# Feed-forward: splits traced behind matmuls, modulation rows traced in the third matrix's products alone, sums of weights on DVE

## The chip, the core and the metric

The kernel runs on one core of a Trainium2 chip. A core has a matrix engine (PE, with a track PEld for its weight loads), a vector engine (DVE), a scalar engine (ACT), GpSimd (POOL) and a sync engine (SP) that here only issues transfers; 16 DMA engines move data between HBM and the on-chip memory. Each engine works through its own queue in order, and waits between engines go over semaphores. The metric is the device time of one execution in microseconds (us), as the median of three runs.

## The reference

Two blocks of two layers each work on 512 tokens of width 1024. The change touches the feed-forward of the second block alone, which runs once per layer `l`. The modulation `mod` of the second layer has 48 columns of 128 numbers; the kernel computes them beside the first layer's feed-forward.

```
mod = (c_act @ ada_w[l] + ada_b[l])[:, None, :]
sh1, sc1, g1, sh2, sc2, g2 = jnp.split(mod, 6, axis=-1)
...
h = rmsnorm_2(x, norm_ffn_g[l]) * (1.0 + sc2) + sh2
f = (jax.nn.silu(h @ ffn_w1[l]) * (h @ ffn_w3[l])) @ ffn_w2[l]
x = x + g2 * f
```

## The kernel before

**Products in three parts.** All products keep float32 precision: each operand is cut into a rounded high part and the rest, and three matmuls are accumulated (high times high, high times low, low times high). A weight tile of 128 by 1024 is loaded to `wraw` by SP, its high part `whi` is made by ACT, and its low part `wlo` by DVE, which subtracts. `Weights` does this along a plan: `load` issues a transfer as soon as a buffer is free, `cut` makes the two parts, and `next` hands the next tile to the products and cuts a few tiles ahead (`depth`, 4 in the feed-forward).

**The feed-forward** (`ffn`). The 22 tiles of the hidden width stand in three groups (`FGROUPS`: tiles 0 to 7, 8 to 15, 16 to 21). For each group the first and third weight matrices (`ffn_w1`, `ffn_w3`) give the hidden tiles `G`, and the second (`ffn_w2`, the "third matrix" of the title, products `w2p`) adds its share to `x`. Tiles 0 and 1 of the first group are multiplied plainly. All others go in pairs through `seven` (L1501): two hidden tiles by two halves of the tokens by two halves of the width are formed from seven products in place of eight. That takes sums of four quarters of the weights. Of these, 8 operations on 128 by 512 are made per pair, 80 per layer, by POOL: `sums12` (L139, L140) writes `wsum`, `sums34` (L147, L148) overwrites parts of `wraw`. Each pair then cuts its weights in seven steps: six of 128 by 1024 (L162 on ACT, L170 on DVE) and one of two halves (L166). ACT copies partial results out of PSUM (`sp`, L1522), and DVE adds them (L1594, L1602), which also sets a PSUM bank free for the next product. A layer has ten pairs: three, four and three.

**Modulation of the second layer** (`ada2_gen`, L480). In the first layer's feed-forward, 48 weight tiles of 128 by 1024 are loaded to `adab` (three buffers), and DVE multiplies each by a broadcast vector and sums along the row. One step of this generator is asked for after each pair and at five of sixteen places of the third matrix's products. SP issues these loads in the same queue as the weights (L477 and L119).

**What sets the order.** The code is traced once; a scheduler then orders each engine's queue, by the place in the trace and by when its own model of the program has an instruction ready. `issue_after(ins)` makes the instructions of a block that belong to the engine of `ins` stand behind `ins` in that engine's queue; it says nothing on instructions of another engine. Blocks around `next(ada)` hang on a matmul, and trace instructions for DVE and for a DMA queue.

Of the kernel before, what the change touches and what calls it, by code (L numbers as in the profile page):

```python
# [14 lines left out]
OP = mybir.AluOpType  # L15
# [60 lines left out]
class Weights:  # L76
# [4 lines left out]

    def __init__(self, nc, raw, split, plan, bufs):
        self.nc, self.raw, self.split, self.bufs = nc, raw, split, bufs
        self.loads, self.cuts, self.sums = [], [], []
# [48 lines left out]
    def sums12(self, n, kc):  # L133

        self.load(n + 2)
        G, w = self.nc.gpsimd, kc * 128
        a, b = self.tiles[n], self.tiles[n + 1]
        st = self.extra.tile([128, 2, w], F32, tag="wsum", bufs=2, name="wsum")
        G.tensor_tensor(st[:, 1], b[:, :w], b[:, w:2 * w], op=OP.add)  # L139
        G.tensor_tensor(st[:, 0], st[:, 1], a[:, :w], op=OP.subtract)  # L140
        self.st[n] = st

    def sums34(self, n, kc):

        G, w = self.nc.gpsimd, kc * 128
        a, b = self.tiles[n], self.tiles[n + 1]
        G.tensor_tensor(a[:, :w], a[:, :w], b[:, :w], op=OP.subtract)  # L147
        G.tensor_tensor(a[:, w:2 * w], a[:, w:2 * w], self.st[n][:, 0], op=OP.subtract)  # L148

# [66 lines left out]
    def next(self, n=None):  # L216
        at = self.n_use
        self.cut(at + (n or self.depth))
        self.load(len(self.loads))
        while self.extra and self.sums and self.sums[0][0] <= at:  # L220
            _, f, m, kc = self.sums.pop(0)
            f(m, kc)
        return self.ready.pop(0)[1:]
# [53 lines left out]
class Kern:  # L277
# [4 lines left out]
    def mm3(self, ps, hi, lo, xh, xl, start, stop):  # L282
        mm = self.nc.tensor.matmul
        mm(ps, hi, xh, start=start, stop=False)  # L284
        mm(ps, hi, xl, start=False, stop=False)  # L285
        return mm(ps, lo, xh, start=False, stop=stop).ins  # L286

# [14 lines left out]
    def run(self):  # L302
        tc, nc, a = self.tc, self.nc, self.a
        with ExitStack() as ctx:
# [11 lines left out]
            self.hx = [hp.tile([128, 8, N], F32R, name=f"hx{i}") for i in range(2)]  # L316
            self.W = Weights(nc, self.wraw, self.wsp, self.weight_plan(), 4)
            self.block1(ctx)
# [134 lines left out]
    def ada2_gen(self, l, bufs=None):  # L453
# [19 lines left out]
        ws = []  # L473
        for f in range(48):
            while len(ws) < min(len(bufs) if bufs else 1, 48 - f):
                w = tile()
                nc.sync.dma_start(w, a["ada_wt2"][l, f + len(ws)])  # L477
                ws.append(w)
# [40 lines left out]
    def dense_halves(self, h, outs):  # L519

        w = [self.W.next(self.W.depth - i) for i in range(len(outs))]
        for o in HALVES:
# [825 lines left out]
class Block2:  # L1348
# [155 lines left out]
    def seven(self, pool, banks):  # L1504
# [7 lines left out]
        def product(ps, b, start):  # L1512
            hi, lo = K.W.next()
            for k in range(4):
                mm(ps, hi[:, k, :], b[0][:, k, :], start=k == 0 and start, stop=False, skip_group_check=True)  # L1515
                mm(ps, hi[:, k, :], b[1][:, k, :], start=False, stop=False, skip_group_check=True)  # L1516
                self.mm_last = mm(ps, lo[:, k, :], b[0][:, k, :], start=False, stop=k == 3, skip_group_check=True).ins  # L1517
                self.step()
# [26 lines left out]
    def ffn(self, l, s):  # L1545
# [18 lines left out]
        for gi, (f0, f1) in enumerate(FGROUPS):  # L1564
            G = [gp.tile([128, 8, N], F32R, tag=f"g{i}", name=f"g{i}") for i in range(2)]
            f = f0
            while f < f1:
                if f < FPLAIN:
                    if f:
                        p1, p3 = self.dense("d"), self.dense("pt")  # L1570
                    else:
                        p1, p3 = (K.pt("fa", "dps") for _ in range(2))
                        for _ in K.dense_halves(self.h, (p1, p3)):
                            self.step()
                    sl = big()
                    A.activation(sl, p1, AF.Silu)
# [32 lines left out]
                K.split(G[0][:, f - f0 + 1, :], G[1][:, f - f0 + 1, :], sl[1])  # L1609
                with self.tc.issue_after(self.mm_last):  # L1610
                    next(ada, None)
                f += 2
# [801 lines left out]
```

## Time and profile before

| | |
|---|---|
| median of three runs | 2543.09 us (2541.26 to 2546.3) |
| profiled execution, its own time | 2536.63 us |
| its span | 2534.8 us |
| PE busy in the span | 2363.8 us, 93% |
| DVE busy | 1934.3 us, 76% |
| ACT busy | 1358.1 us, 54% |
| POOL busy | 508.8 us, 20% |
| HBM read | 255.82 MB, 105 GB/s over the span |

The feed-forward of layer 0 lies from about 1527 to 1914 us of the span, that of layer 1 from about 2165 to 2523 us. The pairs of layer 0 lie from 1554 to 1633, 1678 to 1772 and 1817 to 1878 us, those of layer 1 from 2193 to 2257, 2302 to 2383 and 2427 to 2487 us; the third matrix's products stand between and behind them. A share of busy time is an average over all stages; a stage's limit is read from its own stretch, by which engine is never idle there and by what PE waits for. Matmuls are pipelined, so PE is shown busy also when its clock is lowered.

### The profile page before, as it was taken

The numbers are of one execution on the slowest core, as the hardware profiler recorded it, in microseconds if no ns is written. First come the engines' busy times: TensorE is split into PE (matmuls) and PEld (weight loads), VectorE is DVE, ScalarE is ACT, GpSimd is POOL, SyncE is SP. The second block draws the span as 40 slices with busy tenths as digits, with TensorE's granted clock in tenths as the row PEclk, the third lists the DMA queues.
The fourth block names the chain that finished last, engine by engine and source line by source line (L and its number), as shares of the span: only waits on it lengthen the run. The fifth ranks groups of instructions, "written<-read, shape, count | busy, mean of one in ns | idle before, by whom it ended". The sixth has DMA issues, their size and how long they took to land. (4 is left out here: it accounts for less than half of the span.)

```text
span 2534.8 us, 37905 instructions
## 1 busy us (share of the span) xinstructions
PE 2363.8 (93%) x14392; PEld 2035.2 (80%) x14392; DVE 1934.3 (76%) x3109; ACT 1358.1 (54%) x2656; POOL 508.8 (20%) x366
## 2 busy tenths in 40 slices
PE   7899999999999999999978998898999889899998
PEld 3788888888887888888766777888897578789997
DVE  5778777888367888887589869999477985976765
ACT  4566555667245655577645554435355555544443
POOL 0110000000020000000045105344333520444440
PEclk9999999999999999999988998999999899999999
DMA  6112332234331156523322114674232212232322
GB/s 257 45 55 92 103 101 94 88 98 146 99 95 44 55 176 217 185 76 113 92 72 68 55 59 141 236 255 144 82 100 72 68 56 67 84 125 76 125 72 71
DMA packets 87750, 269.68 MB, mean 106 GB/s; under 512 B 12048, under 2 KB 22544, under 8 KB 87184
## 3 DMA queue, kind: packets, MB, share of 16 engines
q1 hardware_dynamic: 85152, 257.96, 31.4%
q0 software_dynamic: 2416, 9.31, 1.0%
q8 instruction: 113, 1.85, 0.3%
q14 instruction: 69, 0.57, 0.1%
HBM read 255.82 MB, written 11.40 MB: 105 GB/s over the span
## 5 line engine op out<-in xcount | busy, mean ns | idle before, releaser
L284 PE MATMUL dps<-hx,whi 128*128 128x512 f32 (+1 forms) x1040 | 416.1, 400 | 16.2 <-ACT q L1739 5.0
L286 PE MATMUL dps<-hx,wlo 128*128 128x512 f32 (+1 forms) x1040 | 403.9, 388 | 10.9 <-DVE wlo L205 8.5
L285 PE MATMUL dps<-hx,whi 128*128 128x512 f32 (+1 forms) x1040 | 404.3, 389 | 3.2 <-DVE hx L517 2.2
L204 ACT ACTIVATE whi<-wraw 128x1024 fp32r<-128x1024 f32 (+2 forms) x202 | 194.0, 964 | 256.8 <-issue 78.1
L205 DVE TENSOR_TENSOR wlo<-wraw,whi 128x1024 fp32r<-128x1024 f32 (+1 forms) x182 | 225.4, 1239 | 77.4 <-ACT whi L204 75.9
L286 PEld LDWEIGHTS dps<-hx,wlo 128*128 128x128 f32 x1040 | 202.4, 195 | 47.3 <-DVE wlo L205 9.3
L284 PEld LDWEIGHTS dps<-hx,whi 128*128 128x128 f32 x1040 | 203.0, 195 | 45.7 <-DVE t L1762 6.6
L285 PEld LDWEIGHTS dps<-hx,whi 128*128 128x128 f32 x1040 | 202.9, 195 | 28.4 <-DVE hx L517 4.2
L1158 ACT ACTIVATE ph<-PT 128x512 fp32r<-128x512 f32 (+1 forms) x280 | 152.8, 559 | 134.1 <-PE PT L1153 130.7
L1159 DVE TENSOR_TENSOR pl<-PT,ph 128x512 fp32r<-128x512 f32 (+1 forms) x280 | 175.1, 640 | 43.1 <-ACT ph L1158 41.0
L162 ACT ACTIVATE whi<-wraw 128x512 fp32r<-128x512 f32 x200 | 121.0, 626 | 100.9 <-PE w2p L285 35.4
L1141 PE MATMUL Y<-ph,vt 128*128 128x256 f32 (+1 forms) x592 | 161.3, 282 | 6.8 <-DVE T L1175 2.9
L1142 PE MATMUL Y<-pl,vt 128*128 128x256 f32 (+1 forms) x592 | 162.5, 291 | 3.4 <-DVE pl L1159 3.2
L1153 PE MATMUL PT<-ident,P 128*128 128x128 f32 x1024 | 159.5, 275 | 5.9 <-DVE pl L1159 4.0
L1208 POOL DMA_DIRECT2D us<-T x22 | 12.4, 564 | 744.6 <-DVE T L1203 714.2
L284 PE MATMUL w2p<-g,whi 128*128 128x512 f32 (+1 forms) x364 | 140.8, 387 | 1.8 <-ACT sl L1598 1.7
L285 PE MATMUL w2p<-g,whi 128*128 128x512 f32 (+1 forms) x364 | 140.4, 386 | 0.0
L286 PE MATMUL w2p<-g,wlo 128*128 128x512 f32 (+1 forms) x364 | 140.4, 386 | 0.0
L1153 PEld LDWEIGHTS PT<-ident,P 128*128 128x128 f32 x1024 | 118.4, 140 | 23.2 <-DVE pl L1159 9.5
L1141 PEld LDWEIGHTS Y<-ph,vt 128*128 128x128 f32 x592 | 111.7, 189 | 28.6 <-ACT ph L1158 19.7
L170 DVE TENSOR_TENSOR wlo<-wraw,whi 128x1024 fp32r<-128x1024 f32 x80 | 110.3, 1380 | 23.0 <-ACT whi L162 22.7
L1092 PE MATMUL S<-kt,qt 128*128 128x256 f32 (+2 forms) x576 | 125.8, 326 | 1.7 <-DVE nm L1110 0.9
(477 smaller groups left out, 6915.1 us busy)
## 6 DMA issues: line engine op xcount, KB each, us to landing
wraw<-ffn_w SPq DMA_DIRECT2D x120, 512.0 KB, 4.3
wraw<-w_in SPq DMA_DIRECT2D x112, 512.0 KB, 3.5
adaw<-ada_wt SPq DMA_DIRECT2D x80, 512.0 KB, 4.0
adab<-ada_wt SPq DMA_DIRECT2D x48, 512.0 KB, 5.1
wraw<-w_out SPq DMA_DIRECT2D x32, 384.0 KB, 3.1
aw<-ada_w SPq DMA_DIRECT2D x16, 512.0 KB, 10.2
wraw<-w_out SPq DMA_DIRECT2D x16, 512.0 KB, 3.5
bias<-bias_b SPq DMA_DIRECT2D x16, 384.0 KB, 3.5
```

The costliest lines, as they stand in the source:

```text
L162: self.nc.scalar.activation(hi[:, j * w:j * w + w], x, AF.Copy)
L204: s = self.nc.scalar.activation(hi[:, q], t[:, q], AF.Copy)
L205: v = E.tensor_tensor(lo[:, q], t[:, q], fr(hi[:, q]), op=OP.subtract)
L284: mm(ps, hi, xh, start=start, stop=False)
L285: mm(ps, hi, xl, start=False, stop=False)
L286: return mm(ps, lo, xh, start=False, stop=stop).ins
L1092: mm(S[:, so:so + n], Q[:, j, qc], Kt[:, i, ko:ko + n], start=i == 0, stop=i == 1)
L1141: mm(o, v, ph[:, co:co + w], start=b == 0 and n == 0, stop=False, skip_group_check=True)
L1142: mm(o, v, pl[:, co:co + w], start=False, stop=b == len(banks) - 1 and n == len(items) - 1, skip_group_check=True)
L1153: nc.tensor.transpose(pst[:, col:col + 128], ps[t][:, pc:pc + 128], K.ident)
L1158: A.activation(ph[:, :col], pst[:, :col], AF.Copy)
L1159: V.tensor_tensor(pl[:, :col], pst[:, :col], fr(ph[:, :col]), op=OP.subtract)
```

## The change

- The sums of weights (`sums12`, `sums34`) are issued on DVE in place of POOL.
- `next` cuts at most two tiles in front of the products, and the rest of the tiles ahead, with the sums, in a block that hangs on the last matmul. The next loads are traced behind it.
- The first plain tiles cut two tiles in advance and two more at fixed steps of their products.
- The step of the modulation after each pair is gone; the third matrix's products ask for one at six of sixteen places in place of five.
- The modulation's loads in the feed-forward are issued from ACT's queue in place of SP's.

```
@@ -79,8 +79,8 @@
 
 
 
-    def __init__(self, nc, raw, split, plan, bufs):
-        self.nc, self.raw, self.split, self.bufs = nc, raw, split, bufs
+    def __init__(self, K, raw, split, plan, bufs):
+        self.K, self.tc, self.nc, self.raw, self.split, self.bufs = K, K.tc, K.nc, raw, split, bufs
         self.loads, self.cuts, self.sums = [], [], []
         for e in plan:
             n = len(self.loads)
@@ -133,19 +133,19 @@
     def sums12(self, n, kc):
 
         self.load(n + 2)
-        G, w = self.nc.gpsimd, kc * 128
+        V, w = self.nc.vector, kc * 128
         a, b = self.tiles[n], self.tiles[n + 1]
         st = self.extra.tile([128, 2, w], F32, tag="wsum", bufs=2, name="wsum")
-        G.tensor_tensor(st[:, 1], b[:, :w], b[:, w:2 * w], op=OP.add)
-        G.tensor_tensor(st[:, 0], st[:, 1], a[:, :w], op=OP.subtract)
+        V.tensor_tensor(st[:, 1], b[:, :w], b[:, w:2 * w], op=OP.add)
+        V.tensor_tensor(st[:, 0], st[:, 1], a[:, :w], op=OP.subtract)
         self.st[n] = st
 
     def sums34(self, n, kc):
 
-        G, w = self.nc.gpsimd, kc * 128
+        V, w = self.nc.vector, kc * 128
         a, b = self.tiles[n], self.tiles[n + 1]
-        G.tensor_tensor(a[:, :w], a[:, :w], b[:, :w], op=OP.subtract)
-        G.tensor_tensor(a[:, w:2 * w], a[:, w:2 * w], self.st[n][:, 0], op=OP.subtract)
+        V.tensor_tensor(a[:, :w], a[:, :w], b[:, :w], op=OP.subtract)
+        V.tensor_tensor(a[:, w:2 * w], a[:, w:2 * w], self.st[n][:, 0], op=OP.subtract)
 
     def cut_sums(self, at, i, n, kc):
         w = kc * 128
@@ -215,11 +215,17 @@
 
     def next(self, n=None):
         at = self.n_use
-        self.cut(at + (n or self.depth))
+        if self.extra is None:
+            self.cut(at + (n or self.depth))
+        else:
+
+            self.cut(at + min(n or 2, 2))
+            with self.tc.issue_after(self.K.mm_last):
+                self.cut(at + (n or self.depth))
+                while self.sums and self.sums[0][0] <= at:
+                    _, f, m, kc = self.sums.pop(0)
+                    f(m, kc)
         self.load(len(self.loads))
-        while self.extra and self.sums and self.sums[0][0] <= at:
-            _, f, m, kc = self.sums.pop(0)
-            f(m, kc)
         return self.ready.pop(0)[1:]
 
 
@@ -283,7 +289,8 @@
         mm = self.nc.tensor.matmul
         mm(ps, hi, xh, start=start, stop=False)
         mm(ps, hi, xl, start=False, stop=False)
-        return mm(ps, lo, xh, start=False, stop=stop).ins
+        self.mm_last = mm(ps, lo, xh, start=False, stop=stop).ins
+        return self.mm_last
 
     def split(self, hi, lo, src, scale=None):
 
@@ -314,7 +321,7 @@
             self.small = P("small", 3)
             hp = P("hxp")
             self.hx = [hp.tile([128, 8, N], F32R, name=f"hx{i}") for i in range(2)]
-            self.W = Weights(nc, self.wraw, self.wsp, self.weight_plan(), 4)
+            self.W = Weights(self, self.wraw, self.wsp, self.weight_plan(), 4)
             self.block1(ctx)
             self.B2.run()
 
@@ -474,7 +481,7 @@
         for f in range(48):
             while len(ws) < min(len(bufs) if bufs else 1, 48 - f):
                 w = tile()
-                nc.sync.dma_start(w, a["ada_wt2"][l, f + len(ws)])
+                (nc.scalar if bufs else nc.sync).dma_start(w, a["ada_wt2"][l, f + len(ws)])
                 ws.append(w)
             w, o = ws.pop(0), self.junk()
             nc.vector.scalar_tensor_tensor(o, w, 1.0, cb, op0=OP.mult, op1=OP.mult, accum_out=m[:, f:f + 1])
@@ -518,7 +525,7 @@
 
     def dense_halves(self, h, outs):
 
-        w = [self.W.next(self.W.depth - i) for i in range(len(outs))]
+        w = [self.W.next(2 - i) for i in range(len(outs))]
         for o in HALVES:
             for (hi, lo), ps in zip(w, outs):
                 for k in range(8):
@@ -1514,7 +1521,7 @@
             for k in range(4):
                 mm(ps, hi[:, k, :], b[0][:, k, :], start=k == 0 and start, stop=False, skip_group_check=True)
                 mm(ps, hi[:, k, :], b[1][:, k, :], start=False, stop=False, skip_group_check=True)
-                self.mm_last = mm(ps, lo[:, k, :], b[0][:, k, :], start=False, stop=k == 3, skip_group_check=True).ins
+                K.mm_last = mm(ps, lo[:, k, :], b[0][:, k, :], start=False, stop=k == 3, skip_group_check=True).ins
                 self.step()
 
         def copy(src, name):
@@ -1570,8 +1577,11 @@
                         p1, p3 = self.dense("d"), self.dense("pt")
                     else:
                         p1, p3 = (K.pt("fa", "dps") for _ in range(2))
-                        for _ in K.dense_halves(self.h, (p1, p3)):
+                        for i, _ in enumerate(K.dense_halves(self.h, (p1, p3))):
                             self.step()
+                            if i in (17, 25):
+                                with self.tc.issue_after(K.mm_last):
+                                    K.W.cut(K.W.n_split + 1)
                     sl = big()
                     A.activation(sl, p1, AF.Silu)
                     V.tensor_tensor(sl, sl, p3, op=OP.mult)
@@ -1607,8 +1617,6 @@
                     if (t, o) == (0, 1):
                         K.split(G[0][:, f - f0, :], G[1][:, f - f0, :], sl[0])
                 K.split(G[0][:, f - f0 + 1, :], G[1][:, f - f0 + 1, :], sl[1])
-                with self.tc.issue_after(self.mm_last):
-                    next(ada, None)
                 f += 2
 
             if gi == last:
@@ -1620,7 +1628,7 @@
                 for k in range(f1 - f0):
                     v = K.mm3(ps, w[0][:, k, :], w[1][:, k, :], G[0][:, k, o:o + n], G[1][:, k, o:o + n], k == 0,
                               k == f1 - f0 - 1)
-                    if (8 * ct + k) % 16 in (1, 4, 7, 10, 13):
+                    if (8 * ct + k) % 16 in (0, 3, 5, 8, 11, 13):
                         with self.tc.issue_after(v):
                             next(ada, None)
```

What this does to the queues is seen in the order of the instructions. PE's queue has the same order as before. The order on all five queues is row for row the same when the three blocks that hang on a matmul are left out of the changed kernel.

DVE, first pair of layer 0, from the addition that follows the second product to the additions on which PE's last two products wait (`adab`, `junk`: modulation; `wsum`: sums; `wlo`: low parts). Before:

```order
L1594 TENSOR_TENSOR sl<-sfc,sp_15915 128x256
L170 TENSOR_TENSOR wlo<-wraw,whi 128x1024
L467 SCALAR_TENSOR_TENSOR adab<-adab 128x1024
L1602 TENSOR_TENSOR sl<-sy,sp_15949 128x256
L170 TENSOR_TENSOR wlo<-wraw,whi 128x1024
L480 SCALAR_TENSOR_TENSOR junk,mod_9635<-adab 128x1024
L166 TENSOR_TENSOR wlo<-wraw,whi 128x512
L480 SCALAR_TENSOR_TENSOR junk,mod_9635<-adab 128x1024
L166 TENSOR_TENSOR wlo<-wraw,whi 128x512
L480 SCALAR_TENSOR_TENSOR junk,mod_9635<-adab 128x1024
L170 TENSOR_TENSOR wlo<-wraw,whi 128x1024
L1594 TENSOR_TENSOR sl<-sd,sp_15995 128x256
```

And the same place now (L1604 is the former L1594):

```order
L1604 TENSOR_TENSOR sl<-sfc,sp_15915 128x256
L170 TENSOR_TENSOR wlo<-wraw,whi 128x1024
L1612 TENSOR_TENSOR sl<-sy,sp_15949 128x256
L170 TENSOR_TENSOR wlo<-wraw,whi 128x1024
L166 TENSOR_TENSOR wlo<-wraw,whi 128x512 x2
L139 TENSOR_TENSOR wsum<-wraw 128x512
L170 TENSOR_TENSOR wlo<-wraw,whi 128x1024
L140 TENSOR_TENSOR wsum<-wsum,wraw 128x512
L1604 TENSOR_TENSOR sl<-sd,sp_15995 128x256
L1604 TENSOR_TENSOR sl<-spt,sp_15981 128x256
L170 TENSOR_TENSOR wlo<-wraw,whi 128x1024
L139 TENSOR_TENSOR wsum<-wraw 128x512
```

Four modulation operations have left this place, and two sums of half their width stand there; a third sum follows right behind the addition. Counted over DVE's queue between the first addition of one pair and that of the next, the modulation's operations, with the one that prepares the vector, were 5, 6, 7 in the first three pairs, 19 in the products after them, and 6, 6, 0, 0 in the next four. They are now 0, 2, 6, then 18, then 5, 1, 3, 7, and 7 in the products after those. The sums are 8, 8, 0 in the first three pairs, 10 in the products after them, and 6, 8, 8, 0 in the next four.

ACT, fourth pair of layer 0, from its first copy on (`sp`: copies out of PSUM). Before:

```order
L1522 ACTIVATE sp_17024<-sfa 128x256
L162 ACTIVATE whi<-wraw 128x512 x2
L1522 ACTIVATE sp_17058<-sfa 128x256
L162 ACTIVATE whi<-wraw 128x512 x2
L1522 ACTIVATE sp_17090<-sfa 128x256
```

And the same place now:

```order
L1529 ACTIVATE sp_17027<-sfa 128x256
L484 DMA adab<-ada_wt 128x1024
L162 ACTIVATE whi<-wraw 128x512 x2
L1529 ACTIVATE sp_17061<-sfa 128x256
L484 DMA adab<-ada_wt 128x1024
L162 ACTIVATE whi<-wraw 128x512 x2
L1529 ACTIVATE sp_17093<-sfa 128x256
```

A load into one of three buffers stands between two copies of PSUM. Of the 48 loads on ACT, 16 stand among the pairs' copies and 32 in the products of the third matrix (22 after the third pair, 10 after the seventh).

## Rows read from the trace of the kernel before

**Rows 1.** Busy time by stretch: us, engines in turn, clock, DMA share, GB/s.
```profile
1554.00:1633.00 79.00, 66.26 (x504) 64.83 (x503) 77.63 (x93) 39.92 (x80) 38.97 (x20) 0.91 0.60 205
1633.00:1678.00 45.00, 44.69 (x195) 36.50 (x196) 39.26 (x53) 9.86 (x14) 14.29 (x8) 1.00 0.85 285
1678.00:1772.00 94.00, 82.62 (x671) 81.19 (x669) 87.36 (x110) 46.39 (x96) 45.19 (x24) 0.98 0.53 178
1817.00:1878.00 61.00, 60.22 (x505) 59.82 (x504) 50.81 (x56) 34.88 (x72) 25.90 (x14) 1.00 0.32 104
2193.00:2257.00 64.00, 60.54 (x501) 59.65 (x501) 57.49 (x60) 37.69 (x77) 40.12 (x20) 1.00 0.34 109
2302.00:2383.00 81.00, 80.34 (x673) 79.93 (x672) 69.56 (x75) 47.74 (x97) 39.93 (x22) 1.00 0.34 115
```

**Rows 2.** PE groups of the first feed-forward: count, busy, mean ns, idle before, releasers.
```profile
L1515 PE MATMUL sd<-hs,whi 128*128 128x256 f32 x120 | 35.8, 299 | 14.1 <-DVE sl L1594 10.6 <-ACT sp L1522 2.9 <-DVE up L1602 0.5
L1515 PE MATMUL sfa<-hs,whi 128*128 128x256 f32 x120 | 34.9, 291 | 6.5 <-DVE sl L1594 5.7 <-ACT sp L1522 0.8
```

**Rows 3.** Busy time just after the longest of those waits.
```profile
1579.00:1584.00 5.00, 4.54 (x22) 4.54 (x23) 4.11 (x8) 2.90 (x6) 3.63 (x3) 0.52 0.71 262
```

**Rows 4.** Timeline of PE, five waits: start, length, instruction, idle before.
```profile
1535.39 0.39 PE L286 MATMUL dps<-hx,wlo 128*128 128x256 f32 x1 [0.56 <-POOL wlo L205]
...
1555.97 0.39 PE L1517 MATMUL sd<-hx,wlo 128*128 128x256 f32 x1 [1.70 <-DVE wlo L170]
...
1579.46 0.58 PE L1515 MATMUL sd<-hs,whi 128*128 128x256 f32 x1 [4.95 <-DVE sl L1594]
...
2174.78 0.39 PE L286 MATMUL dps<-hx,wlo 128*128 128x256 f32 x1 [1.82 <-POOL wlo L205]
...
2193.94 0.39 PE L1517 MATMUL sd<-hx,wlo 128*128 128x256 f32 x1 [0.94 <-DVE wlo L170]
```

**Rows 5.** DVE groups by shape from 1554 to 1772 us.
```profile
L480 DVE SCALAR_TENSOR_TENSOR junk<-adab 128x1024 bf16<-128x1024 f32 x48 | 67.9, 1414 | 6.4 <-DMA adab<-ada_wt 6.1
L170 DVE TENSOR_TENSOR wlo<-wraw,whi 128x1024 fp32r<-128x1024 f32 x28 | 39.7, 1422 | 3.3 <-ACT whi L162 3.3
L170 DVE TENSOR_TENSOR wlo<-wsum,whi 128x1024 fp32r<-128x1024 f32 x14 | 24.9, 1775 | 0.4 <-ACT whi L162 0.4
L293 DVE TENSOR_TENSOR g<-sl,g 128x512 fp32r<-128x512 f32 x14 | 18.3, 1311 | 0.0
L166 DVE TENSOR_TENSOR wlo<-wraw,whi 128x512 fp32r<-128x512 f32 x14 | 9.0, 679 | 0.0
L1606 DVE TENSOR_TENSOR sl<-sl 128x512 f32<-128x512 f32 x7 | 8.1, 1161 | 0.5
```

**Rows 6.** Timeline of DVE in the first two pairs.
```profile
1574.55 2.31 DVE L480 SCALAR_TENSOR_TENSOR junk<-adab 128x1024 bf16<-128x1024 f32 x1
...
1576.80 2.27 DVE L170 TENSOR_TENSOR wlo<-wraw,whi 128x1024 fp32r<-128x1024 f32 x1
...
1578.99 0.41 DVE L1594 TENSOR_TENSOR sl<-sd,sp 128x256 f32<-128x256 f32 x1
...
1594.10 1.21 DVE L480 SCALAR_TENSOR_TENSOR junk<-adab 128x1024 bf16<-128x1024 f32 x1
...
1599.00 1.28 DVE L166 TENSOR_TENSOR wlo<-wraw,whi 128x512 fp32r<-128x512 f32 x2
```

**Rows 7.** Timeline of POOL: one sum, and one that waits for weights.
```profile
1579.15 1.29 POOL L147 TENSOR_TENSOR wraw<-wraw 128x512 f32<-128x512 f32 x1 [1.16 <-DVE wlo L170]
...
2179.99 1.71 POOL L139 TENSOR_TENSOR wsum<-wraw 128x512 f32<-128x512 f32 x1 [3.55 <-DMA wraw<-ffn_w]
```

**Rows 8.** Timeline of SP: two runs of modulation loads.
```profile
1600.68 18.56 SPq L477 DMA_DIRECT2D adab<-ada_wt  x5
...
1662.14 25.96 SPq L477 DMA_DIRECT2D adab<-ada_wt  x12
```

**Rows 9.** DMA issues of the feed-forward weights: KB each, median us to landing.
```profile
wraw<-ffn_w SPq DMA_DIRECT2D x120, 512.0 KB, 4.3
```

More of the change, by code (lines that the diff above doesn't have):

```diff
@@ L76, with __init__ @@
 class Weights:
-    def __init__(self, nc, raw, split, plan, bufs):
-        self.nc, self.raw, self.split, self.bufs = nc, raw, split, bufs
+    def __init__(self, K, raw, split, plan, bufs):
+        self.K, self.tc, self.nc, self.raw, self.split, self.bufs = K, K.tc, K.nc, raw, split, bufs
         self.loads, self.cuts, self.sums = [], [], []
@@ L135, in sums12 @@
         self.load(n + 2)
-        G, w = self.nc.gpsimd, kc * 128
+        V, w = self.nc.vector, kc * 128
         a, b = self.tiles[n], self.tiles[n + 1]
         st = self.extra.tile([128, 2, w], F32, tag="wsum", bufs=2, name="wsum")
-        G.tensor_tensor(st[:, 1], b[:, :w], b[:, w:2 * w], op=OP.add)
-        G.tensor_tensor(st[:, 0], st[:, 1], a[:, :w], op=OP.subtract)
+        V.tensor_tensor(st[:, 1], b[:, :w], b[:, w:2 * w], op=OP.add)
+        V.tensor_tensor(st[:, 0], st[:, 1], a[:, :w], op=OP.subtract)
         self.st[n] = st
     def sums34(self, n, kc):
-        G, w = self.nc.gpsimd, kc * 128
+        V, w = self.nc.vector, kc * 128
         a, b = self.tiles[n], self.tiles[n + 1]
-        G.tensor_tensor(a[:, :w], a[:, :w], b[:, :w], op=OP.subtract)
-        G.tensor_tensor(a[:, w:2 * w], a[:, w:2 * w], self.st[n][:, 0], op=OP.subtract)
+        V.tensor_tensor(a[:, :w], a[:, :w], b[:, :w], op=OP.subtract)
+        V.tensor_tensor(a[:, w:2 * w], a[:, w:2 * w], self.st[n][:, 0], op=OP.subtract)
     def cut_sums(self, at, i, n, kc):
@@ L217, in next @@
         at = self.n_use
-        self.cut(at + (n or self.depth))
+        if self.extra is None:
+            self.cut(at + (n or self.depth))
+        else:
+            self.cut(at + min(n or 2, 2))
+            with self.tc.issue_after(self.K.mm_last):
+                self.cut(at + (n or self.depth))
+                while self.sums and self.sums[0][0] <= at:
+                    _, f, m, kc = self.sums.pop(0)
+                    f(m, kc)
         self.load(len(self.loads))
-        while self.extra and self.sums and self.sums[0][0] <= at:
-            _, f, m, kc = self.sums.pop(0)
-            f(m, kc)
         return self.ready.pop(0)[1:]
@@ L285, in mm3 @@
         mm(ps, hi, xl, start=False, stop=False)
-        return mm(ps, lo, xh, start=False, stop=stop).ins
+        self.mm_last = mm(ps, lo, xh, start=False, stop=stop).ins
+        return self.mm_last
     def split(self, hi, lo, src, scale=None):
@@ L476, in ada2_gen @@
                 w = tile()
-                nc.sync.dma_start(w, a["ada_wt2"][l, f + len(ws)])
+                (nc.scalar if bufs else nc.sync).dma_start(w, a["ada_wt2"][l, f + len(ws)])
                 ws.append(w)
@@ L519, in dense_halves @@
     def dense_halves(self, h, outs):
-        w = [self.W.next(self.W.depth - i) for i in range(len(outs))]
+        w = [self.W.next(2 - i) for i in range(len(outs))]
         for o in HALVES:
@@ L1572, in ffn @@
                         p1, p3 = (K.pt("fa", "dps") for _ in range(2))
-                        for _ in K.dense_halves(self.h, (p1, p3)):
+                        for i, _ in enumerate(K.dense_halves(self.h, (p1, p3))):
                             self.step()
+                            if i in (17, 25):
+                                with self.tc.issue_after(K.mm_last):
+                                    K.W.cut(K.W.n_split + 1)
                     sl = big()
```

8 lines of the change are left out of this document (3 added, 5 removed).

## The prediction

> **What bounds the kernel now.** I read the busy time by stretch first, because the whole span hides the stage. In the first layer's pairs DVE is the engine that never rests: 77.63 of 79 us in the first group and 87.36 of 94 in the second, with PE at 66.26 and 82.62 [rows 1]. The second layer does the same products in 64 and 81 us, and the third group, which holds no modulation in either layer, takes 61 [rows 1]. So the first layer's first two groups lose 15 and 13 us to something that the second layer's do not have. The groups of PE's waits say what: of 20.6 us idle before the products with summed activations (`hs`), 16.3 end with a DVE addition at L1594 [rows 2]. One wait lasts 4.95 us [rows 4], and in the 5 us after it the granted clock is 0.52, near the lower of the two levels (1.2 of 2.4 GHz) [rows 3]; so a stall is paid again at half speed. That is why PE is "busy" 66.26 us on 504 matmuls which, at the 60.22 us for 505 of the third group, need 60.1.
>
> Why DVE is late is read from its groups by shape. The same cut of 128x1024 takes 1.42 us on loaded weights and 1.78 on sums, and a split of 128x512 takes 1.31 us at L293 but 0.68 at L166 [rows 5]. On the timeline a modulation row takes 2.31 us in one place and 1.21 in another [rows 6]. The long ones lie where POOL makes sums: just before the 4.95 us wait stand a row of 2.31 and a cut of 2.27 us, and the addition that PE waits for begins behind them, at 1578.99 [rows 6]. POOL's instructions and DVE's, both with two inputs from on-chip memory, are in each other's way. DVE is then the engine to count.
>
> **The change part by part.** *The ties to matmuls.* They order nothing: a tie binds instructions of PE's queue alone, the blocks hold work of DVE, ACT and DMA queues, and the order without the ties is the same. No wait on a matmul is added, so I cost the ties at nothing and take only the new order in the queues.
>
> *Sums on DVE, and POOL silent* (1554 to 1772 us, first layer). DVE is busy 77.63 + 39.26 + 87.36 = 204.2 of 218 us [rows 1]. Undisturbed, the shapes take 1.21 [rows 6] and 0.68 us [rows 5]. The excess is 48 x (1.414 - 1.21) = 9.8 for the modulation, 28 x 0.21 = 5.9 and 14 x 0.565 = 7.9 for the cuts, 14 x (1.311 - 0.679) = 8.8 for the splits and 7 x 0.48 = 3.4 for L1606 [rows 5]: 35.8 us that go. By the new order 48 sums stand in DVE's queue there (8, 8, 0, 10, 6, 8, 8, 0). A sum has the shape of the cuts at L166, of which two follow each other in 1.28 us [rows 6], so 48 x 0.64 = 30.7 us come. Seven modulation operations leave for the products at 1772, 7 x 1.21 = 8.5 us. DVE's new work is 204.2 - 35.8 + 30.7 - 8.5 = 190.6 us.
>
> PE needs there 60.1 + 44.7 + 672 x 60.22 / 505 = 80.1, in sum 184.9 us [rows 1]. DVE stays the longer by some 6 us. How much idle it keeps is not in a row; before it had 1.4 + 6.6 us in the two stretches of pairs, and I keep these 8.0: 198.6 us, 19.4 less than 218. Bounds: the second layer's same three stretches, 64 + 45 + 81 = 190, give 28 less; if DVE's order is as unlucky as before, nothing. I stay with 19.4, since DVE's sum is above PE's.
>
> The Trainium skill ("SBUF — State Buffer", Who interferes with whom) says that a DVE instruction with two SBUF inputs and a GpSimd one that reads SBUF exclude each other through one shared interface, held for the whole instruction, rather than slow each other in proportion. The rows agree: 1.21 becomes 2.31 us, a delay of about one undisturbed POOL sum (1.29 us [rows 7]). By the rule at its full price, 52 sums of POOL in the stretch would cost DVE 52 x 1.29 = 67 us and the stretch would fall to the 190 us of the second layer (the first rival below); the groups show only 35.8, because many sums run beside additions out of PSUM, and I keep the groups.
>
> *Second layer, pairs.* The excess per POOL sum above is 35.8 / 52 = 0.69 us; 20 and 22 sums of POOL there give 13.8 and 15.2. DVE goes from 57.5 to 57.5 - 13.8 + 16 x 0.64 = 53.9 us, and from 69.6 to 69.6 - 15.2 + 22 x 0.64 = 68.5, below PE's 60.1 and 80.1. Both stretches become PE's: 3.9 + 0.9 us at most [rows 1]; I take 4, and 0.5 of the third group's 0.8 in the first layer.
>
> *Where the feed-forwards begin.* PE waits there for a cut that POOL makes behind its own sums, 0.56 and 1.82 us, and for DVE's first cut of a pair, 1.70 and 0.94 [rows 4], together 5.0. POOL's queue is now free for its cut; DVE loses its collisions and gains four sums of 0.64 ahead of its own first cut. Between 0 and 5.0; I take 4.
>
> *Added waits: weights.* On POOL a sum that waited for its tile, as the one with 3.55 us [rows 7], held back nobody. On DVE everything queues behind it: additions that free PSUM, and cuts. The second sum of a pair needs a tile whose buffer the seventh cut frees, and a tile lands 4.3 us after its issue [rows 9]. Between that cut and the sum DVE has a half cut, a sum, a cut, a sum, two additions and a cut, 0.64 + 0.64 + 1.21 + 0.64 + 0.82 + 1.21 = 5.2 us, which covers it barely. Some 14 pairs stand so: from 0 to 14 x 3.55 = 50 us; I take 1.
>
> *Added waits: ACT.* A modulation load must wait until DVE has read the buffer's last row. SP, with nothing else to do, held 18.56 us for five and 25.96 for twelve [rows 8], 3.7 and 2.2 us each. ACT holds cuts and the copies of PSUM behind the issue. It is busy 39.92 of 79 and 46.39 of 94 us [rows 1], so it can lose half its time before it counts. 16 issues stand among the pairs: 0 to 16 x 3.71 = 59 us; I take 1, since most stand where the buffer's reader precedes in DVE's queue by several operations. The 22 issues in the products at 1633 lie beside PE work of 44.7 us with cuts made ahead. The Trainium skill ("DMA: Bandwidth & Descriptors", Issuing engines are not separate DMA queues) holds that another issuing engine brings no bandwidth. No run here shows it; by it the 22 loads would go at SP's 2.16 us each, 47.5 us, and that stretch would grow by 2.8.
>
> Sum: -19.4 - 4.5 - 4 + 1 + 1 = -25.9 us, made against the profiled execution (2536.63 us), so 2510.7. The median of the runs before is 6.5 us above that execution; on its scale the forecast is 2517.
>
> **The rivals.** *PE bounds everything.* DVE's remaining idle vanishes in slack carried from the products between, and the stretch takes the second layer's 190: -28 - 4.8 - 5 - 0.8 = -38.6, 2504 us. For it: the second layer, where DVE was busy 90% with collisions and PE lost only 4 us. Against: DVE's sum is above PE's in the first layer, and the fourth and seventh pairs still have 5 and 7 modulation operations.
>
> *DVE waits for weights.* If each of 14 second sums holds the queue for half of 3.55 us, 25 us come back: 2543.1 - 27.9 + 25 = 2540. For it: 5.2 against 4.3 us is a thin cover, with heavier traffic beside. Against: in the second layer DVE has 6 and 12 us to spare.
>
> *ACT's queue closes the circle (slower).* Among the pairs each issue holds ACT for the 3.7 us of SP's worse run, the copies come late, the banks stay full, and DVE idles while ACT waits for DVE. 16 x 3.71 = 59: 2543.1 - 27.9 + 59 = 2574 us. It decides for slower from 27.9 / 16 = 1.7 us per issue on. For it: the load stands directly between two copies in the fourth pair. Against: ACT's free half.
>
> **How the numbers follow.** Forecast 0.62, PE-bound 0.15, DVE waiting for weights 0.13, ACT 0.10. The forecast's own range is 2508 to 2528. The 8-in-10 range is 2499 to 2540: below lies the end of the PE-bound case, above the ACT case and half of the weights' case. A measurement of this kernel tells 0.2%, 5 us, from no change. Forecast and PE-bound are faster, and of the weights' case a half; the rest of that is no change, with a little of it and the ACT case slower: 0.83, 0.07, 0.10.
>
> **What would show it.** L293 at 0.68 and L170 at 1.21 us throughout, the first layer's first group near 64 us and its second near 88, the second layer's first near 60; L1594 as PE's releaser cut to a third or less. It is wrong if DVE's own idle at L139 or L140 behind DMA exceeds 10 us, if ACT's copies become PE's main releaser, or if 128x512 sums take over 1 us on DVE.

## The result and the profile after

The changed kernel takes 2503.65 us, the median of four runs (2502.46 to 2509.49). Before takes 2544.64 us in the same session; the ratio is 0.9851 (95% interval 0.9836 to 0.9866), so 1.5% faster. The forecast was 2517 us in a range of 2499 to 2540. The profiled execution took 2502.77 us, 33.9 less than that of before, where the prediction's sum was 25.9.

First the busy time by stretch of the changed kernel, the answer to [rows 1] (the columns as there: busy time of PE, PEld, DVE, ACT and POOL, each with its count of instructions):

```profile
1553.00:1613.00 60.00, 59.72 (x503) 59.70 (x503) 59.70 (x92) 38.27 (x76) 0.00 (x0) 1.00 0.51 180
1613.00:1657.00 44.00, 44.00 (x194) 35.89 (x193) 41.45 (x63) 9.68 (x13) 0.00 (x0) 1.00 0.89 304
1657.00:1742.00 85.00, 82.22 (x675) 81.74 (x674) 81.69 (x129) 48.19 (x96) 0.00 (x0) 0.98 0.57 196
1786.00:1846.00 60.00, 60.00 (x506) 59.92 (x505) 46.63 (x70) 36.24 (x71) 0.00 (x0) 1.00 0.34 106
2162.00:2224.00 62.00, 60.37 (x504) 59.79 (x503) 54.48 (x82) 37.88 (x75) 0.00 (x0) 1.00 0.36 119
2268.00:2350.00 82.00, 80.90 (x676) 80.42 (x675) 64.66 (x97) 49.24 (x97) 0.00 (x0) 1.00 0.36 116
```

POOL is silent in all of them. The first layer's first group of pairs went from 79 to 60 us, its second from 94 to 85, and PE's clock is 1.00 and 0.98 where it was 0.91 and 0.98 [rows 1]. In the first group PE and DVE each have 0.3 us of gap left. DVE has 284 instructions from 1553 to 1742 us (the first three lines), where it had 256 from 1554 to 1772, and 182.8 us of busy time for 204.2 [rows 1]. Over the whole span DVE is busy 1922.1 us where it was 1934.3, with 160 instructions more. Its groups by shape explain it (1553 to 1742 us, the answer to [rows 5]):

```profile
L487 DVE SCALAR_TENSOR_TENSOR junk<-adab 128x1024 bf16<-128x1024 f32 x38 | 46.5, 1224 | 1.7 <-DMA adab<-ada_wt 1.4
L170 DVE TENSOR_TENSOR wlo<-wraw,whi 128x1024 fp32r<-128x1024 f32 x28 | 34.3, 1224 | 0.5 <-ACT whi L162 0.5
L170 DVE TENSOR_TENSOR wlo<-wsum,whi 128x1024 fp32r<-128x1024 f32 x14 | 17.1, 1223 | 0.0
L148 DVE TENSOR_TENSOR wraw<-wraw,wsum 128x512 f32<-128x512 f32 x14 | 9.7, 691 | 0.0
L300 DVE TENSOR_TENSOR g<-sl,g 128x512 fp32r<-128x512 f32 x14 | 9.6, 691 | 0.0
L139 DVE TENSOR_TENSOR wsum<-wraw 128x512 f32<-128x512 f32 x12 | 8.3, 692 | 3.0 <-DMA wraw<-ffn_w 2.9
L1616 DVE TENSOR_TENSOR sl<-sl 128x512 f32<-128x512 f32 x7 | 4.8, 689 | 0.0
L1616 DVE TENSOR_TENSOR sl<-sl,up 128x256 f32<-128x256 f32 x7 | 2.9, 420 | 0.0
```

Each shape in these rows has one duration now: 1.22 us for 128x1024 whatever it reads (before 1.41, 1.42 and 1.78 [rows 5]), 0.69 for 128x512 (before 1.31 at what was L293). PE's waits before the products with `hs` in the first feed-forward, the answer to [rows 2]:

```profile
L1522 PE MATMUL sfa<-hs,whi 128*128 128x256 f32 x120 | 34.3, 286 | 2.1 <-DVE up L1612 2.1
L1522 PE MATMUL sd<-hs,whi 128*128 128x256 f32 x120 | 34.0, 283 | 0.7 <-DVE up L1612 0.7
```

The 20.6 us are 2.8, and the addition that released most of them (L1594, now L1604) releases none. PE's first waits in each feed-forward, the answer to [rows 4] (timeline of PE):

```profile
1534.80 0.39 PE L292 MATMUL dps<-hx,wlo 128*128 128x256 f32 x1 [0.28 <-POOL wlo L205]
1553.31 0.39 PE L1524 MATMUL sd<-hx,wlo 128*128 128x256 f32 x1 [0.28 <-DVE wlo L170]
2143.97 0.39 PE L292 MATMUL dps<-hx,wlo 128*128 128x256 f32 x1 [0.67 <-POOL wlo L205]
2162.47 0.38 PE L1524 MATMUL sd<-hx,wlo 128*128 128x256 f32 x1 [0.29 <-DVE wlo L170]
```

These four were 0.56, 1.70, 1.82 and 0.94.

### The profile page after: what moved, and what is told of

Same layout as the page of the kernel before. It is cut to its first block, busy times and chain, and to the rows that moved or that the text cites. A ratio compares the mean times of both kernels' runs of the same rounds, so it can differ in the third digit from the quotient of the medians.

```text
span 2501.0 us, 37762 instructions
## 1 busy us (share of the span) xinstructions
PE 2359.8 (94%) x14392; PEld 2034.3 (81%) x14392; DVE 1922.1 (77%) x3269; ACT 1365.9 (55%) x2656; POOL 222.2 (9%) x206
## 3 DMA queue, kind: packets, MB, share of 16 engines
q1 hardware_dynamic: 78240, 232.79, 28.9%
## 5 line engine op out<-in xcount | busy, mean ns | idle before, releaser
L1149 PEld LDWEIGHTS Y<-pl,vt 128*128 128x128 f32 x592 | 111.8, 189 | 13.7 <-DVE pl L1166 6.1
L1118 ACT ACTIVATE P<-P,nm 128x512 f32<-128x512 f32 (+1 forms) x128 | 94.9, 742 | 47.5 <-DVE nm L1117 46.0
```

The source lines that it names most:

```text
L1149: mm(o, v, pl[:, co:co + w], start=False, stop=b == len(banks) - 1 and n == len(items) - 1, skip_group_check=True)
```

## The experiments

The table gives the stages as PE's timeline shows them, each from its first product to the first of the next stage, in us. "Start" is from the end of the last `rrow` product to the first pair. The third matrix's products are left out: in the first layer 44.3 or 44.4 us behind the first two groups and 35.8 or 35.9 behind the third (36.9 in e3, 36.7 in e11).

| stage | before | after | e1 | e2 | e3 | e4 | e5 | e6 | e7 | e8 | e9 | e10 | e11 |
|---|---|---|---|---|---|---|---|---|---|---|---|---|---|
| start, layer 0 | 28.0 | 26.7 | 26.7 | 27.9 | 27.8 | 26.7 | 28.7 | 28.0 | 26.7 | 26.7 | 28.9 | 32.1 | 26.7 |
| start, layer 1 | 28.8 | 26.7 | 26.7 | 28.8 | 30.0 | 26.7 | 28.8 | 28.8 | 26.7 | 26.7 | 30.1 | 33.1 | 26.7 |
| layer 0, pairs 1 | 79.5 | 60.5 | 60.6 | 78.3 | 79.7 | 60.5 | 83.9 | 65.8 | 60.6 | 60.6 | 59.9 | 79.5 | 60.6 |
| layer 0, pairs 2 | 94.7 | 84.7 | 82.3 | 97.6 | 95.2 | 82.5 | 112.8 | 82.1 | 81.6 | 82.1 | 82.2 | 109.3 | 80.1 |
| layer 0, pairs 3 | 61.1 | 59.9 | 60.8 | 61.6 | 62.9 | 60.2 | 75.8 | 70.9 | 60.2 | 60.1 | 59.9 | 72.8 | 59.9 |
| layer 1, pairs 1 | 64.8 | 62.3 | 61.5 | 64.0 | 64.3 | 61.9 | 82.5 | 65.2 | 62.3 | 60.6 | 61.2 | 75.6 | 60.7 |
| layer 1, pairs 2 | 81.0 | 81.3 | 80.8 | 80.8 | 81.4 | 80.7 | 99.0 | 81.4 | 80.1 | 80.1 | 80.2 | 95.8 | 79.9 |
| layer 1, pairs 3 | 60.3 | 59.9 | 59.9 | 59.9 | 60.2 | 59.9 | 67.0 | 60.2 | 59.9 | 60.1 | 59.9 | 67.1 | 59.9 |

**Which part of the change it was.** Three kernels do one part alone, starting from the kernel before.

*e1, the sums on DVE alone* (in `sums12` and `sums34`):

```
-        G, w = self.nc.gpsimd, kc * 128
+        G, w = self.nc.vector, kc * 128
```

> The kernel before, with the 160 sums of weights issued on DVE in place of POOL and nothing else. Theory A (POOL's sums lengthen DVE's operations, 1.21 to 2.31 us; and because the sums fill DVE's queue in the scheduler's model, it moves the modulation out of the pairs by itself): the whole gain, 2503 to 2510 us; in DVE's order the modulation stands 1, 1, 6 in the first three pairs where the kernel before has 5, 6, 7. Theory B (the gain comes from asking for the modulation in the third matrix's products alone): less than half of it, 2520 to 2535. Theory C (cutting ahead in another place of the trace matters): 5 us or more are missing, 2509 and over.

Measured 2501.64 us (2497.07 to 2505.17), ratio 0.9839 (0.9815 to 0.9864). Two changed words give the whole gain. Through the longer queue of DVE they also move the modulation: 1, 1 and 6 operations in the first three pairs, 17 in the products after them.

*e2, the modulation's part alone*: no step after a pair, six of sixteen places, loads on ACT.

```
-                nc.sync.dma_start(w, a["ada_wt2"][l, f + len(ws)])
+                (nc.scalar if bufs else nc.sync).dma_start(w, a["ada_wt2"][l, f + len(ws)])
...
-                with self.tc.issue_after(self.mm_last):
-                    next(ada, None)
...
-                    if (8 * ct + k) % 16 in (1, 4, 7, 10, 13):
+                    if (8 * ct + k) % 16 in (0, 3, 5, 8, 11, 13):
```

> The kernel before, with the modulation's part alone: loads from ACT's queue, no step after a pair, six of sixteen places in the third matrix's products. POOL still makes the sums. Theory A: DVE's order still has 6, 5, 8 modulation operations in the first three pairs and 20 in the products behind them, and the collisions stay: 2538 to 2550 us, no change; waits on ACT for the buffers may cost a few us. Theory B: 2510 to 2525.

Measured 2543.94 us, ratio 1.0001 (0.9991 to 1.0011): nothing. DVE's order still has 6, 5 and 8 modulation operations in the first three pairs, although no step is traced there; a block that hangs on a matmul does not hold DVE's work back.

*e3, the splits ahead alone* (`next` and the plain tiles as in the change, sums on POOL, modulation as before).

> The kernel before, with the splits ahead alone: two tiles cut in front, the rest and the sums traced behind the last matmul, the first plain tiles cut later. POOL makes the sums, the modulation is as before. Theory A: the ties bind nothing and the pairs' queue on DVE hardly moves: 2540 to 2548 us. Theory C: 2530 to 2538.

Measured 2541.58 us, ratio 0.9997 (0.9986 to 1.0009): nothing.

*e4, the changed kernel with the modulation's loads back on SP*:

```
-                (nc.scalar if bufs else nc.sync).dma_start(w, a["ada_wt2"][l, f + len(ws)])
+                nc.sync.dma_start(w, a["ada_wt2"][l, f + len(ws)])
```

> The changed kernel with the modulation's loads back on SP's queue. Theory A: the issues among the pairs cost ACT 0.33 us each without a wait, and SP is idle otherwise; 2501 to 2507 us, the same as the changed kernel (2503.7). Theory D (SP's queue held the weights back, so ACT's issuing is part of the gain): 2509 or more, with weights landing later and DVE waiting for them.

Measured 2501.59 us, ratio 0.9835 (0.9812 to 0.9858), the same as the changed kernel: the issues on ACT cost nothing that can be measured.

**Collisions or only the order.** In e1 the collisions go and the modulation leaves the first pairs; two causes in one edit. *e5* gives the collisions back: e1, with POOL making a sum of weights that nobody reads beside each of DVE's.

```
+            self.nc.gpsimd.tensor_tensor(g, b[:, :w], b[:, w:2 * w], op=OP.add)   # 160 times
```

> Sums on DVE as in e1_sums, and POOL makes a useless sum of the same two halves of the weights beside each of the 160 (its result, in bfloat16 for room, is read by nobody; the output stays the reference's). DVE's order is that of e1_sums. Theory A1 (POOL's reading itself lengthens DVE's operations, wherever they stand): the excess of some 38 us per layer-0 stretch is back on top of DVE's own sums; first layer's groups over 85 and 95 us, second layer's first two over 66 and 82; in all 2540 to 2565 us. Theory A2 (what matters is that the modulation left the pairs in the order): 2500 to 2510 us, as e1_sums.

Measured 2620.23 us, ratio 1.0312 (1.0291 to 1.0334): 119 us above e1 and far beyond what I expected. DVE's queue has e1's order row for row in the feed-forwards, so the order is not the cause. DVE now carries the sums and the collisions. Its waits come back to PE in the first feed-forward:

```profile
L1522 PE MATMUL sd<-hs,whi 128*128 128x256 f32 x120 | 38.1, 317 | 23.3 <-DVE sl L1601 11.2 <-DVE up L1609 6.1 <-ACT sp L1529 5.9
L1522 PE MATMUL sfa<-hs,whi 128*128 128x256 f32 x120 | 35.6, 297 | 14.8 <-DVE up L1609 6.9 <-DVE sl L1601 4.8 <-ACT sp L1529 3.2
```

The useless sums also hold weight buffers longer, so this size was not yet the collisions' alone. *e10* lets POOL add two constant tables instead, behind a read of 128x1 that keeps the pace; *e9* lets it write only.

```
+            self.nc.gpsimd.tensor_tensor(g[:, :1], b[:, :1], b[:, w:w + 1], op=OP.add)        # e9 and e10
+            self.nc.gpsimd.memset(g, 0.0)                                                     # e9
+            self.nc.gpsimd.tensor_tensor(g, self.K.B2.ct, self.K.B2.st, op=OP.add)            # e10
```

> The kernel with the weights' sums on DVE alone, and beside each sum POOL makes a 128x1 read that paces it and one 128x512 sum of two constant float tables, with a result that nobody reads: two operands read as by the sums before, but no weight buffer is held for longer than the 128x1 read. If the collisions alone made the useless sums of weights cost 119 us (theory), the time is 2590 to 2625 us here too; if a good part of that came from weight buffers that came free later and DMAs that started later (rival), it is 2535 to 2575 us.

> The kernel with the weights' sums on DVE alone, and beside each sum POOL makes an element-wide read (128x1) that paces it and a memset of 128x512 that nobody reads, so POOL is as often at work in a pair as before but writes only. If what stretched DVE's instructions was POOL reading two SBUF operands (my theory), DVE's plain times stay (cut 1224, sum 1223, g 691 ns) and the time is that of the sums alone, 2498 to 2508 us. If any work of POOL beside DVE costs DVE time (rival), the pairs come back to 65 to 80 us and the time to 2530 or more.

e10 measured 2605.71 us, ratio 1.0259 (1.024 to 1.0277): 104 of the 119 us come back although a weight buffer is held only until a read of 128x1. By the table 94 us of it lie in the pairs, where e5 has 115, so the collisions are the main cause there; the other 21 fit the buffers, which is not tested. Another 12 us lie in the starts, where POOL's own cut stands behind its useless sums. e9 measured 2504.64 us, ratio 0.9858 (0.9842 to 0.9875), near the time without POOL: its pairs are as short as e1's, and its starts are 2.2 and 3.4 us longer, since POOL's cut waits there too. DVE's groups with POOL adding constants (e10, 1550 to 1740 us):

```profile
L489 DVE SCALAR_TENSOR_TENSOR junk<-adab 128x1024 bf16<-128x1024 f32 x30 | 40.7, 1356 | 3.2 <-DMA adab<-ada_wt 3.1
L179 DVE TENSOR_TENSOR wlo<-wraw,whi 128x1024 fp32r<-128x1024 f32 x22 | 31.0, 1411 | 0.0
L179 DVE TENSOR_TENSOR wlo<-wsum,whi 128x1024 fp32r<-128x1024 f32 x10 | 17.6, 1764 | 0.0
L149 DVE TENSOR_TENSOR wraw<-wraw 128x512 f32<-128x512 f32 x10 | 13.3, 1329 | 0.0
```

and with POOL writing (e9, the same stretch):

```profile
L488 DVE SCALAR_TENSOR_TENSOR junk<-adab 128x1024 bf16<-128x1024 f32 x37 | 45.1, 1218 | 4.2 <-DMA adab<-ada_wt 3.9
L178 DVE TENSOR_TENSOR wlo<-wraw,whi 128x1024 fp32r<-128x1024 f32 x28 | 34.0, 1216 | 0.1
L178 DVE TENSOR_TENSOR wlo<-wsum,whi 128x1024 fp32r<-128x1024 f32 x14 | 17.0, 1216 | 0.0
L148 DVE TENSOR_TENSOR wraw<-wraw 128x512 f32<-128x512 f32 x14 | 9.6, 685 | 0.0
```

while POOL was at work there (e9, POOL's groups from 1553 to 1780 us):

```profile
L155 POOL TENSOR_TENSOR ghost<-wraw 128x1 bf16<-128x1 f32 x56 | 33.9, 605 | 158.9 <-DMA wraw<-ffn_w 155.3
L156 POOL MEMSET ghost<- 128x512 bf16 x56 | 29.4, 524 | 3.3
```

The same DVE instructions of 128x1024 take 1.36 to 1.76 us on average where POOL sums constants, much as where it summed weights before [rows 5], and 1.22 where it writes. A cut of a sum is hit most (1.76). POOL is at work for less time in e9, but single instructions say the same: of the 40 cuts of sums, 22 ran beside a memset and none took over 1.23 us. Whether a POOL instruction that reads one operand would disturb DVE is not tested. The Trainium skill ("SBUF — State Buffer", Who interferes with whom) says that a DVE instruction with two SBUF inputs contends with a GpSimd instruction that reads SBUF and not with one that only writes it; both halves agree with these runs (up to 2.33 us in e10, 1.22 in e9).

**Is it enough to move the modulation?** *e6*: before, sums on POOL, the steps hung on DVE's own instructions, so that they hold: none in the first two groups' pairs, three per pair in the third.

```
+                        if (t, o) == (0, 1):
+                            with self.tc.issue_after(dv):
+                                for _ in range((0, 0, 3)[gi]):
+                                    next(ada, None)
...
-                with self.tc.issue_after(self.mm_last):
-                    next(ada, None)
...
-                        with self.tc.issue_after(v):
+                        with self.tc.issue_after(self.dv):
```

> The kernel before, POOL still making the sums, but the modulation's operations are hung on DVE's own instructions (the addition before them), so that they cannot be moved up into the pairs: 0, 0, 3 in the first three pairs, 17 behind them, 0, 0, 0, 3, then 17, and 3 in each pair of the third group. Theory A2: as good as the changed kernel, 2500 to 2510. Theory A1 in its mild form (collisions and modulation overload DVE together, and either alone fits beside PE, as the second layer's 64.8 and 81.0 us show): the first layer's groups fall from 79.5 and 94.7 to about 65 and 81, 2513 to 2522 us in all. A1 in its strong form (collisions alone keep PE waiting): 2530 or more.

Measured 2527.68 us, ratio 0.9944 (0.9926 to 0.9963), about a third of the gain and between the two ranges that I expected. The busy time by stretch of this kernel (the three groups of pairs of layer 0):

```profile
1554.50:1620.30 65.80, 61.46 (x483) 59.77 (x482) 60.89 (x61) 42.52 (x82) 38.97 (x20) 0.97 0.32 107
1664.50:1746.70 82.20, 81.31 (x662) 80.00 (x661) 74.58 (x79) 45.36 (x93) 50.05 (x26) 1.00 0.38 122
1791.00:1862.00 71.00, 64.53 (x487) 63.29 (x486) 62.36 (x73) 33.41 (x69) 34.47 (x18) 0.93 0.51 161
```

The two groups without rows fell to 65.8 and 82.1 us, with POOL summing all the time. The third group, which got them, rose from 61 to 71. So the collisions without the rows cost some 2 us over PE's floor in the second group and 6 in the first, and with three rows per pair 10 us more than before in the third: DVE does not stand both. That it matters less which of the two is removed than that DVE's sum falls below PE's is my reading; no run shows it by itself.

**What is left behind the change.** *e7* is e1 with the steps hung on DVE instructions and spread: 1, 2 and 3 per pair in the three groups, four of sixteen places in the products. *e8* is e1 with the second pair of first sums made one cut later, so that its tile has landed. *e11* is both.

```
+                                for _ in range((1, 2, 3)[gi]):                                      # e7, e11
+                                    next(ada, None)
...
-    ((-4, self.sums12, 0), (-2, self.sums12, 2), (-1, self.sums34, 0), (0, self.sums34, 2))
+    ((-4, self.sums12, 0), (-1, self.sums12, 2), (-1, self.sums34, 0), (0, self.sums34, 2))         # e8, e11
```

> e1_sums with the modulation hung on DVE's own instructions and spread: 1, 1, 3 in the first three pairs, 14 behind them, 2, 2, 2, 3, then 15, and 3 in two pairs of the third group. If what is left in the second group (82.3 to 84.7 us against 80 for PE) comes from the 4 to 7 modulation operations in its first and last pair: that group at 80 us and 2496 to 2500 in all. If it comes from waits for weights or from PE itself: 2501, the same as e1_sums.

> e1_sums with the second pair of first sums asked for one cut later. In the changed kernel DVE idles 14.0 us at L139 for weights in the second layer and 5.3 in the first. If that wait is what keeps the second layer's first group at 61.5 to 62.3 us against PE's 60: the wait under 5 us, that group at 60 and 2497 to 2500 in all. If the wait is covered by DVE's spare time: less idle at L139 and the same time, 2501, and additions or cuts late by the sum could cost 1 to 3 us.

> The kernel with the weights' sums on DVE alone, the modulation tied to DVE's instructions and spread one to three to a pair, and the second pair of first sums one cut later. The pairs of layer 0 are 60.6, 81.6 and 60.2 us with the first of these alone, and PE's own work is 184.9 us in the first two groups and the product between. If PE is the bound in all of them (theory), nothing is left to gain: 2498 to 2504 us, within 0.2% of the sums alone. If DVE's waits for weights still cost (rival, some 18 us idle in layer 1 before the first cuts), the time falls below 2497 us.

e7 measured 2502.13 us, ratio 0.9842 (0.9821 to 0.9863); e8 2503.47, 0.9852 (0.983 to 0.9873); e11 2497.2 (2494.2 to 2500.52), 0.9829 (0.9811 to 0.9847). Singly they do nothing that the time shows: e7's second group stayed at 81.6 us, not the 80 expected if the rows in its pairs were what is left, and e8 brought the second layer's first group to 60.6 us without a shorter total. Together they have the lowest median of all, 6.5 us below the changed kernel; against before in the same session the difference is 0.2%, the intervals of the ratios overlap, and I call it no more than the best version so far. Its time lies between the two that were expected (2498 to 2504, or below 2497) and does not decide between them. Its stretches of pairs in layer 0 (e11):

```profile
1555.00:1616.00 61.00, 60.58 (x507) 60.30 (x506) 57.59 (x87) 38.53 (x77) 0.00 (x0) 1.00 0.50 165
1660.00:1740.00 80.00, 80.00 (x671) 79.72 (x671) 71.20 (x110) 47.33 (x95) 0.00 (x0) 1.00 0.50 163
1785.00:1845.00 60.00, 60.00 (x506) 59.91 (x505) 53.04 (x86) 35.76 (x72) 0.00 (x0) 1.00 0.43 140
```

PE has at most 0.4 us of gap left at full clock and DVE has 3 to 9 us to spare in each: the floor that PE sets here, 60, 80 and 60 us, is reached in both layers (table). In the pairs, more can come only from PE's own work.

## Why the prediction was right, and which term was mis-sized

By the stages, forecast against measured (a sum of table rows and the products between):

| step of the prediction | forecast, us | measured, us |
|---|---|---|
| layer 0, pairs 1 to pairs 2 | -19.4 | 218.6 to 189.4: -29.2 |
| layer 1, pairs; layer 0, pairs 3 | -4.5 | -2.5 + 0.4 - 0.4 - 1.2 = -3.7 |
| starts | -4 | -1.2 - 2.1 = -3.3 |
| waits for weights, ACT | +2 | within the rows above |
| sum | -25.9 | -36.2 |

Of the 36.2 us, 2.9 came back between the two feed-forwards (250.2 to 253.1 us), where the change touches nothing; e2 and e3, which differ from before in nothing that the time shows, have 252.8 and 252.7 there, and all the others 251.2 to 254.5, so I take this for scatter between executions.

*The mechanism held.* DVE was the bound, POOL's sums stretched it, and the stretch went. e5 and e10 show it by putting it back, e9 by showing that POOL's work as such is harmless. The ties and the splits ahead were costed at nothing and the loads on ACT at 1 us, and e3 and e4 agree. That rows of the modulation leave the stretch, 8.5 us of the sum, came about without the modulation's part as well: e1 moves them too, and e2 alone gains nothing.

*The mis-sized term* is "DVE stays the longer by some 6 us", 190.6 of DVE's work against PE's 184.9, with 8.0 of idle on top. DVE's measured work is 59.70 + 41.45 + 81.69 = 182.8 us and its idle in the pairs 0.30 + 3.31 = 3.6. There is also a slip in the sum: 198.6 us hold no idle time of DVE in the products between the pairs, while the 218 us they are taken from hold 45 - 39.26 = 5.7 [rows 1]. With it kept, as the other idle was, the step would have been 13.7 us and not 19.4. Measured, it is 2.6, and 182.8 + 3.6 + 2.6 = 189.0 us is the whole stretch. So the work was put 7.8 us and the idle in the pairs 4.4 us too high, the slip made up for 2.6 of that, and that the sum came as near as it did is in part luck.

In the work three things were missed. Two groups of before were left out of the excess (DVE by shape, 1554 to 1772 us, mean ns before the last bar):

```profile
L1606 DVE TENSOR_TENSOR sl<-sl,up 128x256 f32<-128x256 f32 x7 | 5.2, 740 | 0.3
...
L467 DVE SCALAR_TENSOR_TENSOR adab<-adab 128x1024 f32<-128x1024 f32 x1 | 2.3, 2306 | 0.0
```

They are 0.420 and 1.23 us now, so 7 x 0.32 + 1.1 = 3.3 us more excess. Then 38 modulation rows stand in the stretch, not 41: 3 x 1.22 = 3.7 us. Against that, 52 sums lie in it, not 48, but DVE begins one 0.60 us after the other (timeline of DVE, first pairs, the answer to [rows 6]):

```profile
1574.46 0.69 DVE L147 TENSOR_TENSOR wraw<-wraw 128x512 f32<-128x512 f32 x1
1575.07 0.69 DVE L148 TENSOR_TENSOR wraw<-wraw,wsum 128x512 f32<-128x512 f32 x1
1575.67 0.69 DVE L300 TENSOR_TENSOR g<-sl,g 128x512 fp32r<-128x512 f32 x1
...
1586.15 1.23 DVE L487 SCALAR_TENSOR_TENSOR junk<-adab 128x1024 bf16<-128x1024 f32 x1
```

52 x 0.60 = 31.2, 0.5 more than reckoned. 190.6 - 3.3 - 3.7 + 0.5 = 184.1, of the measured 182.8; the last 1.3 are not settled. So over the three stretches together DVE fell just below PE instead of just above it, and the condition of the first rival held: its 2504 us is what came, and the argument against it ("DVE's sum is above PE's") was the error. The second layer's 190 us for the same three stretches, named as the lower bound, was the better value, though not stage by stage: they came as 60.5 + 44.3 + 84.7 where the second layer had 64 + 45 + 81. In the second group DVE still works longer (81.69 us) than PE needs (80.1), so PE does not bound everything yet. And the rival's 38.6 us stand against 33.9 between the profiled executions; only the medians, 41.0 us apart, meet its 2504 so closely. A forecast that hangs on a difference of 6 in 190 between two engines should give the other side more than 0.15.

*The wait for weights* (second rival) exists. DVE's first sums by layer (1526 to 1850, and 2135 to 2400 us; idle time before them behind the second bar):

```profile
L139 DVE TENSOR_TENSOR wsum<-wraw 128x512 f32<-128x512 f32 x20 | 13.8, 691 | 5.4 <-DMA wraw<-ffn_w 5.3
...
L139 DVE TENSOR_TENSOR wsum<-wraw 128x512 f32<-128x512 f32 x17 | 11.8, 692 | 14.2 <-DMA wraw<-ffn_w 14.0
```

The 14.0 us are above the 10 that the prediction named as a sign against it. They stand in the second layer, where DVE has 7.5 of 62 and 17.3 of 82 us free, and reach PE only as 2.4 us of waits on L1612 there; in e8, with the later sum, none of these are left, and against e1, from which e8 differs in that sum alone, the stages are 0.9 and 0.7 us shorter. The expected cost of 1 us was of the right size, the sign too coarse: idle time of an engine counts only where that engine has no slack.

*The circle through ACT* (third rival) did not close, and [rows 8] is why it had to be asked. Timeline of ACT at three places, one in the products and two among the pairs:

```profile
1618.84 5.65 ACTq L484 DMA_DIRECT2D adab<-ada_wt  x3
...
1659.06 0.34 ACTq L484 DMA_DIRECT2D adab<-ada_wt  x1
1659.50 1.16 ACT L162 ACTIVATE whi<-wsum 128x512 fp32r<-128x512 f32 x2 [4.13 <-DVE junk L487]
...
1665.12 1.15 ACT L162 ACTIVATE whi<-wraw 128x512 fp32r<-128x512 f32 x2 [2.45 <-DVE junk L487]
```

An issue takes 0.33 us where its buffer is free. Where it is not, ACT stands behind it until DVE has read the last row: it idles 4.13 us up to 1659, with two loads in them, 2.45 us up to 1665, and up to 1.9 us a load in the runs among the products. No load among the pairs held it for the rival's 3.7 us. The products did not grow by 2.8 us either; they took 44.3 us, as with the loads on SP (e4). And ACT is busy only 38 of 60 us and 48 of 85, and its copies are not among what PE waits for. The one wait over 1 us that PE has in the second group begins just behind such places (2.12 us at 1678, on DVE); with the loads on SP that group is 82.5 us against 84.7, with the rows spread 81.6. Whether the 2.2 us are ACT's is not settled, since the total time of e4 is the same.

## What to carry to other kernels

Before engines are balanced by counting work, compare the durations of one shape across places: where a DVE instruction has two durations, look at what runs beside it. Here it was POOL reading two operands, and taking over that work made DVE's queue shorter. Where two engines come out within a few per cent of each other, count every group, from start to start rather than by duration, and idle time in every stretch; the stage's floor is the slower engine. A block that hung on an instruction of another engine moved nothing here (e2): to place DVE's work, hang it on DVE.

## What was not expected of the hardware

- POOL's writes cost DVE nothing (1.22 us beside memsets), its sums of two operands up to 1.1 us per instruction: in e10, 25 of the 40 cuts of 128x1024 on a sum take 1.98 to 2.33 us (median 2.26) and the other 15 take 1.21 to 1.23.
- DVE's additions out of PSUM are not disturbed: in the kernel before, the 15 on `spt` that ran wholly beside a POOL sum took 0.41 us, as the others did.
- The collisions cost both sides: POOL's sum took 1.29 us beside such additions [rows 7], and 1.80 to 1.96 us on average in the same stretch of before.
- DVE starts the next instruction before the profile ends the last: 0.60 us from start to start for 0.69 of duration.
- 160 sums that nobody needs, each with a read of 128x1, cost 104 us on an engine that had little else to do (e10 against e1).
